# Six Strassen groups a layer instead of four, their split differences in slots of their own, and a 512-wide first product in every Strassen tile

## The chip, the cores and the metric

The kernel runs on one core of a Trainium2 chip. The time is that of one execution in device microseconds; the median of three executions of the kernel before is 1974.74 us (1974.21 to 1976.4). The core has a matrix engine (PE, which multiplies, and whose weight loads the profile lists apart as PEld), a vector engine (DVE), a scalar engine (ACT), GpSimd (POOL) and SyncE (SP), which here issues the loads of the weights.

## The reference, cut to what matters

Two layers over 256 tokens of width 2048: a recurrent block or an attention block, and behind each a SwiGLU block, the part that the change touches:

```python
D_MODEL = 2048; SEQ = 256
D_FF = 5632

def swiglu_ffn(x, g, w_in, w_out):
    h = rms_norm(x, g)
    gate, up = jnp.split(h @ w_in, 2, axis=-1)
    return x + (jax.nn.silu(gate) * up) @ w_out
```

All is float32. The kernel multiplies in a narrower format and keeps float32 precision by splitting each operand in a high and a low part and adding three products: high x high, high x low, low x high.

## The kernel before, in words

**Jobs.** The program is one list of jobs, one for each 512 KB tile of weights (256 rows by 512 columns). `stream` (line 321) walks through it: SP loads the tile of job i+4 into one of four `raw` buffers, ACT writes its high part `hi` and DVE its low part `lo` three jobs ahead (`split`, lines 295 to 310), and the job then issues its matmuls. `hi0..3`, `lo0..3` are here called the ring. The order of a job list and of the work between jobs (generators stepped by `run_bg` against budgets for DVE and ACT) is fixed when the program is built.

**Plain jobs** (`group`, `products`, matmul on line 375) have a ring tile as weights and the activations as moving operand; the activations (high and low part, 256 tokens each) lie in slots `s`. A plain job is 24 matmuls, each 256 columns wide. In groups whose output has a PSUM bank for itself, high x high and high x low can be issued as one matmul 512 wide whose two halves are added later; `products` does so in runs of three (a job then has 21 matmuls, three of them wide).

**Strassen jobs** (`strassen`, matmul on line 476) serve the first `NS` = 4 of the 22 groups of the SwiGLU input projection, eight jobs each. Operands are exchanged: the activations are the weights of the array, and the tile of the layer's weights moves. A job forms 7 products of 256 columns instead of 8, with three matmuls each: 21. Three products take a quarter of the ring tile as it is (`B(1)`, `B(3)`, `B(2)`); four take the differences t1 to t4, which POOL computes (`sums`, lines 279 to 281), ACT and DVE split in high and low two jobs ahead (`split_sums`, lines 289 and 291), and which lie in two sets of six slots taken from the pool of 58. In the first and last job of a group the products stand in the order of `todo`; in the six between, the three plain ones come first. Behind the eighth job `fast` (line 675) adds up the four banks on DVE, `task` applies SiLU and issues four transposes on PE through `pe_other` (lines 383 and 386), and `later` keeps the result back until the layer's last Strassen job is issued.

**Order of the jobs of one layer's input projection** (end of `ffn`): 8 plain jobs, then one Strassen job and two plain jobs in turn, then the rest of the plain ones; behind them the output projection. While they alternate, the plain jobs are of the kind without wide matmuls.

The weights are laid out for the Strassen groups on the host by `quarters`, with `NS` groups. Elsewhere in the program, the job of the shared K/V (lines 1052 to 1063) has twelve matmuls with operands as in a plain job, then twelve with operands exchanged as in a Strassen job.

Of the kernel before, what the change touches and what calls it, by code (L numbers as in the profile page):

```python
# [12 lines left out]
F32 = mybir.dt.float32  # L13
F32R = mybir.dt.float32r
AF = mybir.ActivationFunctionType
ALU = mybir.AluOpType

P = 128
D = 2048
T = 256  # L20
DFF = 5632
ND = D // P
# [19 lines left out]
class Val:  # L42


    def __init__(self, ap=None):
        self.ap = ap
        self.ready = False


class Trunk:  # L50
# [15 lines left out]
    DVE_TICK = 640.0  # L66
    ACT_TICK = 800.0

    NS = 4
    AHEAD = 8  # L70
    OWN = 2
    LS = 2
# [2 lines left out]
    def __init__(self, ctx, tc, dram):  # L75
        self.tc, self.nc, self.d = tc, tc.nc, dram
        nc = self.nc
        const = ctx.enter_context(tc.tile_pool(name="const", bufs=1))
        psum = ctx.enter_context(tc.tile_pool(name="psum", bufs=1, space=bass.MemoryType.PSUM))
        tmp = ctx.enter_context(tc.tile_pool(name="tmp", bufs=1))  # L80
        self.tmp = tmp
        self.par = const.tile([P, NPAR], F32, name="par")
        self.con = const.tile([P, NCON], F32, name="con")
        self.cc = const.tile([P, 32], F32, name="cc")
        self.x = [const.tile([P, 4, T], F32, name=f"x{i}") for i in range(4)]
        self.slots = deque(range(58))
        self.spool = const
        self.held = {}
        self.raw = [const.tile([P, 1024], F32, name=f"raw{i}") for i in range(4)]
        self.hi = [const.tile([P, 1024], F32R, name=f"hi{i}") for i in range(4)]  # L90
        self.lo = [const.tile([P, 1024], F32R, name=f"lo{i}") for i in range(4)]
        self.banks = deque(psum.tile([P, 512], F32, name=f"b{i}") for i in range(8))
        self.misc = 0
        self.started = False
        self.xin = 0
        self.other = None
        self.summing = False
        self.opening = None
        self.sets = None
        self.runs = 0  # L100
        self.since = 0
        self.hold = False
        self.tmps = deque(const.tile([P, T], F32, name=f"t{i}") for i in range(4))
        self.halves = deque(const.tile([P, T], F32, name=f"h{i}") for i in range(8))
        self.rstd = [const.tile([P, T + 2], F32, name=f"rstd{i}") for i in range(2)]
        self.acc = const.tile([P, T], F32, name="acc")
        self.sq = deque(const.tile([P, T], F32, name=f"sq{i}") for i in range(2))
        self.jobs = []
        self.bg = deque()
        self.tick = -2 * self.LD  # L110
        self.dve = 0.0
        self.act = 0.0
# [17 lines left out]
    def tt(self, out, a, b, op):  # L130
        self.dve += 69 + 1.042 * self._n(out)
        self.nc.vector.tensor_tensor(out, a, b, op)  # L132
# [14 lines left out]
        self.nc.vector.reciprocal(out, a)  # L147


    def slot(self, dt=F32R):  # L150
        i = self.slots.popleft()
        s = self.spool.tile([P, 2 * T], dt, tag=f"s{i}", name=f"s{i}")
        self.held[id(s)] = (i, s)
        return s

    def free(self, s):
        self.slots.append(self.held.pop(id(s))[0])

    def half(self):
        if self.halves:  # L160
# [108 lines left out]
    def sums(self, i):  # L269

        raw, tt = self.raw[i % 4], self.nc.gpsimd.tensor_tensor
        if not self.sets:
            self.sets = deque([self.slot(F32), self.slot(F32)] + [self.slot() for _ in range(4)] for _ in range(2))
        s = self.sets.popleft()
        self.sets.append(s)
        self.jobs[i][2]["set"] = s
        b = raw[:, :].rearrange("p (b t) -> p b t", b=4)
        two = lambda q: q.rearrange("p (b t) -> p b t", b=2)
        tt(two(s[0][:, :]), b[:, 0:3:2, :], b[:, 1::-1, :], ALU.subtract)  # L279
        tt(s[1][:, 0:T], raw[:, 2 * T:3 * T], s[0][:, 0:T], ALU.subtract)  # L280
        tt(s[1][:, T:2 * T], raw[:, 3 * T:4 * T], s[1][:, 0:T], ALU.subtract)  # L281
# [39 lines left out]
    def stream(self):  # L321
        n = len(self.jobs)
        self.warm()
        for i in range(-self.LD, n):
            self.tick = 2 * i
            if i + self.LD < n:
                self.load(i + self.LD)
            if 0 <= i + self.LC < n:
                self.split(i + self.LC)
            if 0 <= i + self.LS < n:  # L330
                self.split_sums(i + self.LS)
            if i >= 0:
                self.jobs[i][1](self.hi[i % 4], self.lo[i % 4])
            else:
                self.half_tick()
            self.run_bg()
        self.drain()
# [108 lines left out]
    def strassen(self, src, xs, forms, done, last, left):  # L446

        st = {}
        jobs = []
        for c in range(ND // 2):  # L450
            part = {}

            def mm(hi, lo, c=c, part=part):
                if c == 0:
                    st["ps"] = [self.bank() for _ in range(4)]
                    st["begun"] = set()
                ps = st["ps"]
                x2 = [self.need(xs[2 * c + kt]) for kt in range(2)]
                fh, fl = self.need(forms[c])
                A = lambda kt, b: tuple(x2[kt][:, q + b * P:q + b * P + P] for q in (0, T))  # L460
                S = lambda n: tuple(q[:, n * P:n * P + P] for q in (fh, fl))
                B = lambda n: tuple(q[:, n * T:n * T + T] for q in (hi, lo))
                s = part["set"]
                t1, t3, t2, t4 = (tuple(s[n + q][:, h * T:h * T + T] for q in (0, 1)) for n in (2, 4) for h in range(2))
                todo = [(0, 0, A(0, 0), B(1)), (1, 1, A(1, 0), B(3)), (1, 0, S(1), t2), (2, 0, S(0), t1),
                        (2, 1, S(2), t3), (3, 0, S(3), B(2)), (3, 1, A(1, 1), t4)]
                if 0 < c < ND // 2 - 1:
                    todo = [todo[q] for q in (0, 1, 5, 3, 4, 2, 6)]
                if self.other is not None:
                    self.runs = self.RUNS  # L470
                    self.other = None
                for n, (b, h, w, m) in enumerate(todo):
                    if n == 4:
                        self.half_tick()
                    for i, j in ((0, 0), (0, 1), (1, 0)):
                        self.nc.tensor.matmul(ps[b][:, h * T:h * T + T], w[i], m[j], start=b not in st["begun"],  # L476
                                              stop=c == ND // 2 - 1 and i == 1, skip_group_check=True)
                        st["begun"].add(b)
                        self.since += 1
                left[0] -= 1  # L480
                if last and c == ND // 2 - 1:
                    for q in self.sets:
                        for t in q:
                            self.free(t)
                    self.sets = None
                if last:
                    for q in (fh, fl):
                        self.free(q)
                if c == ND // 2 - 1:
                    done(ps)  # L490
            jobs.append((src(c), mm, part))
        return jobs

# [160 lines left out]
    def ffn(self, l, xs, forms, r, gains, rn, out=None):  # L654
        hid = [Val() for _ in range(NH)]
        w = self.d[f"ffn_in{l}"]
        one = self.con[:, K_ID:K_ID + P]
        turns, ordinary = [], []
        left = [self.NS * ND // 2]

# [12 lines left out]

        for g in range(self.NS):
            def fast(ps, g=g):
                c1, U, V = self.t(), self.slot(F32), self.slot(F32)
                two = lambda q: q.rearrange("p (b t) -> p b t", b=2)
                twice = lambda q: q.unsqueeze(1).broadcast_to([P, 2, T])
                self.a(c1, ps[0][:, 0:T])
                self.tt(two(U[:, :]), two(ps[1][:, :]), twice(c1[:, :]), ALU.add)  # L680
                self.tt(two(V[:, :]), two(ps[2][:, :]), twice(U[:, 0:T]), ALU.add)
                self.tt(U[:, 0:T], ps[2][:, 0:T], V[:, T:2 * T], ALU.add)
# [4 lines left out]
                def task():  # L687
# [23 lines left out]
                    yield from later(g, s)  # L711
                self.spawn(task())
            turns += self.strassen(lambda c, g=g: w[g, c], xs, forms, fast, g == self.NS - 1, left)
        for g in range(self.NS, NH // 2):
            def done(ps, g=g):
# [4 lines left out]
                def task():  # L720
# [28 lines left out]
                    if both is not None:  # L749
                        yield from later(g, both)  # L750
                self.spawn(task())
            self.group(lambda c, g=g: w[g, c], ND, xs, done, g == NH // 2 - 1, self.SYNC,
                       paired=2 * (g <= (self.OWN + 1) * self.NS), jobs=ordinary)
        n = len(turns)
# [618 lines left out]
```

## Time and profile before

| | |
|---|---|
| median of three executions | 1974.74 us |
| the profiled execution's own time | 1976.51 us |
| its span | 1974.7 us |
| granted TensorE clock | 1.00 (share of full speed) |
| PE, PEld busy | 100%, 98% |
| DVE, ACT, POOL busy | 72%, 57%, 19% |
| weights read | 372 MB, 189 GB/s over the span |

Matmuls overlap, so the mean duration of one in the page (282 ns for line 476) is not what it adds to the time. What it adds is the distance from its start to the next start; the chain of work that ended last gives it, where a piece of n matmuls follows another without a gap. A row of the chain reads: start in us, length in us, engine, tile, line, number of instructions.

### The profile page before, as it was taken

What the parts mean: (1) busy time and instruction counts of PE and PEld (TensorE: products, weight loads), DVE (VectorE), ACT (ScalarE), POOL (GpSimd) and SP (SyncE); (2) the same over time, 40 slices, a digit from 0 to 9 for tenths busy, and PEclk for the clock granted to TensorE, in tenths of its full rate; (3) what the DMA queues carried; (4) which work ended last, traced back from release to release, by engine and by line L of the source; (5) the groups of instructions that cost most, each with busy time, mean ns of one, the idle gap of its engine ahead of it and who ended that gap; (6) DMA issues with size and microseconds to landing.
All of it is one profiled execution on the core that took longest, in us unless ns stands there. A gap on an engine that the chain in (4) does not pass through costs nothing.

```text
span 1974.7 us, 40978 instructions
## 1 busy us (share of the span) xinstructions
PE 1966.7 (100%) x16762; PEld 1934.6 (98%) x16762; DVE 1428.8 (72%) x2073; ACT 1121.2 (57%) x1746; POOL 383.4 (19%) x356
## 2 busy tenths in 40 slices
PE   9999999999999999999999999999999999999999
PEld 9999999999999999999999889999999999999999
DVE  8988978988986655545668767888889665554443
ACT  6798766555555444434556776655556554444442
POOL 0000125555520000000002454354444000000000
PEclk9999999999999999999999999999999999999999
DMA  8555665665555555555555434565555656556664
GB/s 276 187 190 177 200 209 193 187 208 197 192 201 191 195 193 192 193 193 196 195 185 182 129 129 152 191 214 193 193 193 201 194 193 193 194 196 205 206 205 127
DMA packets 106204, 377.16 MB, mean 191 GB/s; under 512 B 11936, under 2 KB 14368, under 8 KB 106016
## 3 DMA queue, kind: packets, MB, share of 16 engines
q1 hardware_dynamic: 105408, 373.88, 57.7%
q8 instruction: 131, 2.15, 0.4%
q10 hardware_dynamic: 608, 0.66, 0.1%
q14 instruction: 57, 0.47, 0.1%
HBM read 371.88 MB, written 2.10 MB: 189 GB/s over the span
## 4 chain that ended last, share of the span: by engine, by line
PE 96%; DVE 2%; ACT 1%; issue 0%; POOL 0%; DMA 0%; ACTq 0%; DVEq 0%; POOLq 0%
PE b L375 84%; PE b L476 8%; PE b L386 1%; PE b L866 1%; PE b L383 1%; ACT s L123 1%; DVE lo L309 1%; PE b L1052 1%; ACT hi L306 0%; DVE s L1120 0%; DVE s L132 0%; DMA x<-in_x 0%; PE b L1061 0%; PE b L1062 0%; PE b L1063 0%
## 5 line engine op out<-in xcount | busy, mean ns | idle before, releaser
L375 PE MATMUL b<-s,hi 128*128 128x256 f32 (+1 forms) x9536 | 1301.0, 282 | 1.6 <-ACT s L123 1.0
L375 PEld LDWEIGHTS b<-s,hi 128*128 128x128 f32 x9536 | 1203.1, 188 | 21.4 <-ACT s L123 1.7
L309 DVE TENSOR_TENSOR lo<-raw,hi 128x1024 fp32r<-128x1024 f32 (+1 forms) x643 | 812.5, 1266 | 447.4 <-ACT hi L306 444.8
L306 ACT ACTIVATE hi<-raw 128x1024 fp32r<-128x1024 f32 (+1 forms) x643 | 676.0, 1054 | 588.6 <-PE b L375 508.1
L375 PE MATMUL b<-s,lo 128*128 128x256 f32 x4992 | 748.3, 277 | 0.0
L375 PEld LDWEIGHTS b<-s,lo 128*128 128x128 f32 x4992 | 651.0, 188 | 0.5
L279 POOL TENSOR_TENSOR s<-raw 128x512 f32<-128x512 f32 x64 | 120.8, 1888 | 233.3 <-DMA raw<-in_ffn_in 185.6
L291 DVE TENSOR_TENSOR s<-s,s 128x512 fp32r<-128x512 f32 x128 | 141.5, 1141 | 0.6 <-ACT s L289 0.3
L1142 POOL TENSOR_TENSOR s<-s 128x128 f32<-128x128 f32 x32 | 14.7, 462 | 537.0 <-ACT s L123 534.3
L476 PE MATMUL b<-s,s 128*128 128x256 f32 x768 | 105.6, 282 | 0.5 <-DVE s L291 0.5
L299 ACT ACTIVATE hi<-raw 128x768 fp32r<-128x768 f32 x64 | 54.1, 845 | 78.8 <-PE b L375 56.5
L476 PEld LDWEIGHTS b<-s,s 128*128 128x128 f32 x768 | 97.3, 189 | 0.8 <-DVE s L291 0.7
L123 ACT ACTIVATE s<-s 128x256 fp32r<-128x256 f32 (+3 forms) x180 | 69.1, 429 | 33.4 <-POOL s L508 19.5
L132 DVE TENSOR_TENSOR s<-s,s 128x256 fp32r<-128x256 f32 (+3 forms) x148 | 70.6, 509 | 19.8 <-ACT s L123 19.7
L476 PE MATMUL b<-hi,s 128*128 128x256 f32 x384 | 80.7, 281 | 0.0
L280 POOL TENSOR_TENSOR s<-raw,s 128x256 f32<-128x256 f32 x64 | 78.7, 1230 | 5.0
L300 DVE TENSOR_TENSOR lo<-raw,hi 128x768 fp32r<-128x768 f32 x64 | 70.5, 1102 | 12.6 <-PE b L375 8.1
L289 ACT ACTIVATE s<-s 128x512 fp32r<-128x512 f32 x128 | 73.6, 617 | 7.8 <-POOL s L281 7.8
L506 POOL TENSOR_TENSOR s<-s 128x128 f32<-128x128 f32 x16 | 14.0, 877 | 328.8 <-ACT s L123 328.8
L281 POOL TENSOR_TENSOR s<-raw,s 128x256 f32<-128x256 f32 x64 | 70.9, 1108 | 5.0
L476 PEld LDWEIGHTS b<-hi,s 128*128 128x128 f32 x384 | 64.6, 189 | 0.0
L123 ACT ACTIVATE s<-x,par 128x256 fp32r<-128x256 f32 (+1 forms) x112 | 52.6, 498 | 19.9 <-DVE x L132 13.5
(121 smaller groups left out, 1127.4 us busy)
## 6 DMA issues: line engine op xcount, KB each, us to landing
raw<-in_ffn_in SPq DMA_DIRECT2D x352, 512.0 KB, 3.5
raw<-in_ffn_out SPq DMA_DIRECT2D x176, 512.0 KB, 3.4
raw<-in_lru_in SPq DMA_DIRECT2D x62, 512.0 KB, 3.6
raw<-in_lru_out SPq DMA_DIRECT2D x32, 512.0 KB, 3.8
raw<-in_w_q SPq DMA_DIRECT2D x32, 512.0 KB, 3.4
raw<-in_w_o SPq DMA_DIRECT2D x32, 512.0 KB, 3.3
raw<-in_gate SPq DMA_DIRECT2D x8, 512.0 KB, 3.7
raw<-in_kv SPq DMA_DIRECT2D x8, 512.0 KB, 3.4
```

The source lines that it names most:

```text
L123: self.nc.scalar.activation(out, in_, func, **kw)
L132: self.nc.vector.tensor_tensor(out, a, b, op)
L279: tt(two(s[0][:, :]), b[:, 0:3:2, :], b[:, 1::-1, :], ALU.subtract)
L280: tt(s[1][:, 0:T], raw[:, 2 * T:3 * T], s[0][:, 0:T], ALU.subtract)
L281: tt(s[1][:, T:2 * T], raw[:, 3 * T:4 * T], s[1][:, 0:T], ALU.subtract)
L289: self.nc.scalar.activation(a, z, AF.Copy)
L291: self.nc.vector.tensor_tensor(b, z, a.bitcast(F32), ALU.subtract)
L300: low = self.nc.vector.tensor_tensor(lo[:, q], raw[:, q], hi[:, q].bitcast(F32), ALU.subtract)
L306: high = self.ins(self.nc.scalar.activation(hi[:, q], raw[:, q], AF.Copy))
L309: low = self.nc.vector.tensor_tensor(lo[:, q], raw[:, q], hi[:, q].bitcast(F32), ALU.subtract)
L375: self.nc.tensor.matmul(*args, **kw)
L476: self.nc.tensor.matmul(ps[b][:, h * T:h * T + T], w[i], m[j], start=b not in st["begun"], stop=c == ND // 2 - 1 and i == 1, skip_group_ch ...
```

## The change: what it does

Three things. `NS` goes from 4 to 6, so per layer 48 instead of 32 jobs are Strassen jobs, and 128 instead of 144 plain. The eight slots of the split differences come from a deque of their own (`odd`), which lies in memory right behind the ring, while the pool shrinks from 58 to 57 slots; `hi` and `lo` of a ring tile become the two halves of one tile `part`. All tiles keep their address modulo 512 bytes but these eight: the slots `s` begin at 32 modulo 512, the ring and now the eight slots at 480. The room comes from a scratch area at the start of the memory, which goes from 16 KB to 2 KB a partition. And the first product of a Strassen job, high x high and high x low, is one matmul 512 wide into both halves of its bank; `fast` adds the halves with one more DVE operation.

```diff
--- before.py
+++ after.py
@@ -66,7 +66,10 @@
     DVE_TICK = 640.0
     ACT_TICK = 800.0
 
-    NS = 4
+    NS = 6
+    SLOTS = 57
+    ODD = 8
+    SCRATCH = 2048
     AHEAD = 8
     OWN = 2
     LS = 2
@@ -83,12 +86,15 @@
         self.con = const.tile([P, NCON], F32, name="con")
         self.cc = const.tile([P, 32], F32, name="cc")
         self.x = [const.tile([P, 4, T], F32, name=f"x{i}") for i in range(4)]
-        self.slots = deque(range(58))
+        self.slots = deque(range(self.SLOTS))
+        self.odd = deque(range(self.SLOTS, self.SLOTS + self.ODD))
         self.spool = const
         self.held = {}
         self.raw = [const.tile([P, 1024], F32, name=f"raw{i}") for i in range(4)]
-        self.hi = [const.tile([P, 1024], F32R, name=f"hi{i}") for i in range(4)]
-        self.lo = [const.tile([P, 1024], F32R, name=f"lo{i}") for i in range(4)]
+        self.parts = [const.tile([P, 2, 1024], F32R, name=f"part{i}") for i in range(4)]
+        self.hi, self.lo = ([q[:, h, :] for q in self.parts] for h in range(2))
+        for i in self.odd:
+            const.tile([P, 2 * T], F32R, tag=f"s{i}", name=f"s{i}")
         self.banks = deque(psum.tile([P, 512], F32, name=f"b{i}") for i in range(8))
         self.misc = 0
         self.started = False
@@ -147,14 +153,15 @@
         self.nc.vector.reciprocal(out, a)
 
 
-    def slot(self, dt=F32R):
-        i = self.slots.popleft()
+    def slot(self, dt=F32R, odd=False):
+        i = (self.odd if odd else self.slots).popleft()
         s = self.spool.tile([P, 2 * T], dt, tag=f"s{i}", name=f"s{i}")
         self.held[id(s)] = (i, s)
         return s
 
     def free(self, s):
-        self.slots.append(self.held.pop(id(s))[0])
+        i = self.held.pop(id(s))[0]
+        (self.slots if i < self.SLOTS else self.odd).append(i)
 
     def half(self):
         if self.halves:
@@ -270,7 +277,7 @@
 
         raw, tt = self.raw[i % 4], self.nc.gpsimd.tensor_tensor
         if not self.sets:
-            self.sets = deque([self.slot(F32), self.slot(F32)] + [self.slot() for _ in range(4)] for _ in range(2))
+            self.sets = deque([self.slot(F32), self.slot(F32)] + [self.slot(F32R, True) for _ in range(4)] for _ in range(2))
         s = self.sets.popleft()
         self.sets.append(s)
         self.jobs[i][2]["set"] = s
@@ -330,6 +337,7 @@
             if 0 <= i + self.LS < n:
                 self.split_sums(i + self.LS)
             if i >= 0:
+                self.i = i
                 self.jobs[i][1](self.hi[i % 4], self.lo[i % 4])
             else:
                 self.half_tick()
@@ -462,6 +470,7 @@
                 B = lambda n: tuple(q[:, n * T:n * T + T] for q in (hi, lo))
                 s = part["set"]
                 t1, t3, t2, t4 = (tuple(s[n + q][:, h * T:h * T + T] for q in (0, 1)) for n in (2, 4) for h in range(2))
+                pair = self.parts[self.i % 4][:, :, T:2 * T]
                 todo = [(0, 0, A(0, 0), B(1)), (1, 1, A(1, 0), B(3)), (1, 0, S(1), t2), (2, 0, S(0), t1),
                         (2, 1, S(2), t3), (3, 0, S(3), B(2)), (3, 1, A(1, 1), t4)]
                 if 0 < c < ND // 2 - 1:
@@ -472,7 +481,12 @@
                 for n, (b, h, w, m) in enumerate(todo):
                     if n == 4:
                         self.half_tick()
-                    for i, j in ((0, 0), (0, 1), (1, 0)):
+                    if n == 0:
+                        self.nc.tensor.matmul(ps[0][:, :].rearrange("p (b t) -> p b t", b=2), w[0], pair,
+                                              start=c == 0, stop=c == ND // 2 - 1, skip_group_check=True)
+                        st["begun"].add(0)
+                        self.since = 0
+                    for i, j in ((0, 0), (0, 1), (1, 0))[2 * (n == 0):]:
                         self.nc.tensor.matmul(ps[b][:, h * T:h * T + T], w[i], m[j], start=b not in st["begun"],
                                               stop=c == ND // 2 - 1 and i == 1, skip_group_check=True)
                         st["begun"].add(b)
@@ -676,7 +690,8 @@
                 c1, U, V = self.t(), self.slot(F32), self.slot(F32)
                 two = lambda q: q.rearrange("p (b t) -> p b t", b=2)
                 twice = lambda q: q.unsqueeze(1).broadcast_to([P, 2, T])
-                self.a(c1, ps[0][:, 0:T])
+                self.a(c1, ps[0][:, T:2 * T])
+                self.tt(c1, ps[0][:, 0:T], c1, ALU.add)
                 self.tt(two(U[:, :]), two(ps[1][:, :]), twice(c1[:, :]), ALU.add)
                 self.tt(two(V[:, :]), two(ps[2][:, :]), twice(U[:, 0:T]), ALU.add)
                 self.tt(U[:, 0:T], ps[2][:, 0:T], V[:, T:2 * T], ALU.add)
@@ -1360,7 +1375,8 @@
         arr[f"ffn_in{l}"] = quarters(tiles(wi), Trunk.NS)
         arr[f"ffn_out{l}"] = tiles(ffn_w_out[l])
 
-    nc = bacc.Bacc("TRN2", target_bir_lowering=False, num_devices=1)
+    nc = bacc.Bacc("TRN2", target_bir_lowering=False, num_devices=1,
+                   dynamic_dma_scratch_size=Trunk.SCRATCH)
     dram = {n: nc.dram_tensor(f"in_{n}", v.shape, F32, kind="ExternalInput").ap() for n, v in arr.items()}
     dram["out"] = nc.dram_tensor("out_y", (P, ND, T), F32, kind="ExternalOutput").ap()
     with tile.TileContext(nc) as tc:
```

On PE, one Strassen job of the first layer stood so before (line, operation, output bank <- operands, columns; `hi_77` and `lo_81` are a ring tile, `s_38xx` split differences, the other `s` activations), in the rows up to the first products with a difference:

```order
L375 MATMUL b_84<-s_3262,lo_80 128x256 x2
L476 MATMUL b_85<-hi_77,s_3211 128x256
L476 MATMUL b_85<-lo_81,s_3211 128x256
L476 MATMUL b_85<-hi_77,s_3211 128x256
L476 MATMUL b_86<-hi_77,s_3225 128x256
L476 MATMUL b_86<-lo_81,s_3225 128x256
L476 MATMUL b_86<-hi_77,s_3225 128x256
L476 MATMUL b_88<-hi_77,s_3334 128x256
L476 MATMUL b_88<-lo_81,s_3334 128x256
L476 MATMUL b_88<-hi_77,s_3335 128x256
L476 MATMUL b_87<-s_3869,s_3334 128x256
```

The same place of the changed program (`part_76` is the ring tile with both parts):

```order
L383 MATMUL b_88<-s_3525,part_75 128x256 x2
L485 MATMUL b_89<-part_76,s_3249 128x512
L490 MATMUL b_89<-part_76,s_3249 128x256
L490 MATMUL b_90<-part_76,s_3266 128x256 x3
L490 MATMUL b_92<-part_76,s_3342 128x256 x2
L490 MATMUL b_92<-part_76,s_3343 128x256
L490 MATMUL b_91<-s_3879,s_3342 128x256
```

Two matmuls of 256 columns have become one of 512; the order of the products is the same.

On DVE, between two Strassen groups of the second layer, the rows from the low part of a plain tile before `fast` to the split of the differences for the next group's first job were (`b` is a bank of the group that has ended):

```order
L300 TENSOR_TENSOR lo_79<-raw_71,hi_75 128x768
L132 TENSOR_TENSOR s_16079<-b_90,t_91 128x512
L132 TENSOR_TENSOR s_16080<-b_83,s_16079 128x512
L132 TENSOR_TENSOR s_16079<-b_83,s_16080 128x256
L132 TENSOR_TENSOR s_16080<-b_86,s_16080 128x512
L309 TENSOR_TENSOR lo_80<-raw_72,hi_76 128x1024
L136 SCALAR_TENSOR_TENSOR s_16080<-s_16080,rstd_104,s_16079 128x256
L136 SCALAR_TENSOR_TENSOR s_16079<-s_16079,rstd_104,s_16080 128x256
L291 TENSOR_TENSOR s_14591<-s_14588,s_14590 128x512
L291 TENSOR_TENSOR s_14593<-s_14589,s_14592 128x512
```

In the changed program they are:

```order
L307 TENSOR_TENSOR part_75<-raw_71,part_75 128x768
L138 TENSOR_TENSOR t_97<-b_91,t_97 128x256
L138 TENSOR_TENSOR s_16139<-b_88,t_97 128x512
L138 TENSOR_TENSOR s_16140<-b_94,s_16139 128x512
L138 TENSOR_TENSOR s_16139<-b_94,s_16140 128x256
L138 TENSOR_TENSOR s_16140<-b_92,s_16140 128x512
L316 TENSOR_TENSOR part_76<-raw_72,part_76 128x1024
L142 SCALAR_TENSOR_TENSOR s_16140<-s_16140,rstd_108,s_16139 128x256
L142 SCALAR_TENSOR_TENSOR s_16139<-s_16139,rstd_108,s_16140 128x256
L298 TENSOR_TENSOR s_14666<-s_14663,s_14665 128x512
L298 TENSOR_TENSOR s_14668<-s_14664,s_14667 128x512
```

One operation of 256 columns is added at the head of `fast`; all else follows in the same order. In the second layer four transposes stand inside the first Strassen job of the next group, before and after; in the first layer they stood inside the second plain job ahead of the second Strassen job, and now stand right ahead of the first one.

## The prediction

> **What bounds the kernel now.** I read the page's busy times and chain first, then the chain of the stretch in which Strassen and plain jobs alternate, piece by piece.
>
> ```profile
> PE 1966.7 (100%) x16762; PEld 1934.6 (98%) x16762; DVE 1428.8 (72%) x2073; ACT 1121.2 (57%) x1746; POOL 383.4 (19%) x356
> PE 96%; DVE 2%; ACT 1%; issue 0%; POOL 0%; DMA 0%; ACTq 0%; DVEq 0%; POOLq 0%
> ```
>
> PE is busy all the time and carries 96% of the chain, so what counts is how many matmuls PE issues and how far apart. Here is the chain of the first layer around the boundary between two Strassen groups:
>
> ```profile
> 421.28 2.49 PE b L476 x21
> 423.77 5.44 PE b L375 x48
> 429.22 2.49 PE b L476 x21
> 431.71 5.44 PE b L375 x48
> 437.15 2.48 PE b L476 x21
> 439.63 5.65 PE b L375 x48
> 445.29 2.46 PE b L476 x21
> 447.75 4.25 PE b L375 x36
> 451.99 0.11 PE b L383
> 452.10 0.33 PE b L386 x3
> 452.43 1.42 PE b L375 x12
> 453.85 2.45 PE b L476 x21
> ```
>
> No piece waits for another engine, yet matmuls of equal width differ. A plain job's step is 5.44/48 = 113.3 ns. A Strassen job's is 2.49/21 = 118.6 ns. And behind the last job of a group (439.63) and its successor's first (447.75) the same plain jobs take 5.65/48 = 117.7 ns and 4.25/36 = 118 ns, until the next Strassen job. So a stream of matmuls runs at a short step (113.3) or at a long one (118), and a Strassen job can hand over either. The job of the shared K/V shows the rule without the differences. Twelve matmuls with weights from the ring (L1052) alternate with twelve with the ring as the moving operand (L1061 to L1063):
>
> ```profile
> 1011.28 0.12 PE b L1061
> ...
> 1012.69 1.41 PE b L1052 x12
> 1014.11 0.12 PE b L1061
> ...
> 1015.48 1.36 PE b L1052 x12
> 1016.84 0.12 PE b L1061
> ...
> 1018.26 1.41 PE b L1052 x12
> ```
>
> From start to start, the exchanged twelve take 1.41 us (long step), 1.37 (short), 1.42 (long), and the plain twelve behind them 1.41, 1.36, 1.41. So both kinds can run at the short step, the plain stream inherits the step of the exchanged one, and passing from plain to exchanged flips it. In a Strassen job only 9 of 21 matmuls are of the exchanged kind; in 12 both operands lie in slots. After the change all are exchanged, as far as the place modulo 512 bytes goes.
>
> **The change part by part.** The sum is made against the profiled execution, 1976.5 us with a span of 1974.7, 1.8 us above the median of the runs shown.
>
> *Fewer and dearer jobs.* Per layer 16 plain jobs become Strassen jobs. 32 x 2.72 us (half of 5.44) = 87.0 us go. The old 64 Strassen jobs cost 64 x 2.48 = 158.7 us (five of a group's eight at 2.49, the others 2.48, 2.46, 2.45). The new price needs a wide matmul, which stands in the chain only in plain jobs, three in this piece:
>
> ```profile
> 33.12 5.56 PE b L375 x46
> ```
>
> 5.56 - 43 x 0.1133 = 0.69 us, 0.23 each. No row has one with exchanged operands; bounds are two narrow ones, 0.227 at the short step and 0.237 at the long one, +-0.5 us over 96 jobs. At the short step a job is 0.23 + 19 x 0.1133 = 2.38 us and 96 of them 228.7. Net: -87.0 - 158.7 + 228.7 = **-17.0 us**.
>
> *The plain jobs at the long step.* At a boundary they cost 0.21 + 0.17 + 0.06 = 0.44 us over the short one. That is three boundaries a layer and the two jobs behind the last Strassen job: 6 x 0.44 + 2 x 0.21 = **-3.1 us** if every Strassen job now hands over the short step. The whole stretch agrees:
>
> ```profile
> 316.94:567.99 251.06, 251.06 (x2174) 251.00 (x2173) 229.06 (x249) 143.30 (x208) 133.72 (x91) 1.00 0.60 196
> 567.99:791.00 223.01, 223.01 (x1869) 219.04 (x1868) 135.77 (x189) 108.12 (x145) 0.00 (x0) 1.00 0.59 195
> ```
>
> 62 plain jobs at 2.72, 32 Strassen jobs at 2.48 and three times 0.44 us for the transposes (452.43 - 451.99) make 249.3; the 1.7 us left are the stretch's plain jobs at the long step.
>
> Does one wide matmul bring the job to the short step? It takes twice the time of a narrow one for one weight load, so what the loads lag behind the matmuls in the plain stream should be gone when the second product starts; the exchanged twelve at 1014.11 show that exchanged operands can then stay at it. The range is between the short step everywhere and the long one everywhere: 19 + 48 matmuls at +4.5 ns, 0.30 us a Strassen job, 29 us in all. I take the short step, the end to which the K/V rows with exchanged operands (1.37) and their plain heirs (1.36) are nearest.
>
> A rule speaks against the placement. The Trainium skill says, on "TensorE: Matmul & The Clock Gate", section "Step-by-step: what each phase is for", that loading the next tile's weights "doesn't steal SBUF read bandwidth from the running matmul", over two independent read ports. By it, where the operands lie could change nothing, and the steps above would be equal; the trace disagrees (118.6 against 113.3 ns at one width), but it doesn't say which of place, order and width is the cause.
>
> *Four more groups.* Each brings four transposes, 0.44 us with the restart: **+1.8 us**.
>
> *DVE at the boundary.* `fast` has one more DVE operation. The rows of a boundary in the second layer, DVE and then the chain:
>
> ```profile
> 1336.26 1.95 DVE L132 TENSOR_TENSOR s<-b,s 128x512 f32<-128x512 f32 x3
> 1338.12 1.89 DVE L309 TENSOR_TENSOR lo<-raw,hi 128x1024 fp32r<-128x1024 f32 x1
> 1339.93 1.83 DVE L136 SCALAR_TENSOR_TENSOR s<-s,rstd,s 128x256 f32<-128x256 f32 x2
> 1341.69 1.28 DVE L291 TENSOR_TENSOR s<-s,s 128x512 fp32r<-128x512 f32 x2
> 1344.03 1.41 DVE L132 TENSOR_TENSOR h<-b,rstd 128x256 f32<-128x256 f32 x4
> ```
> ```profile
> 1336.77 5.65 PE b L375 x48
> 1342.43 1.46 PE b L476 x12
> ```
>
> DVE works through without a gap and ends the differences of the next group's first job at 1341.69 + 1.28 = 1342.97. PE needs the second pair after six matmuls, at 1342.43 + 0.71 = 1343.14: 0.17 us to spare. The added operation costs 0.35 us (a quarter of 1.41), and PE arrives 0.21 us earlier (5.44 for 5.65). The wait is then 0.35 + 0.21 - 0.17, some 0.4 us; I take 0.5 at each of five boundaries, +2.5. Queued on PE behind the waiting product are the rest of its job and two plain jobs; all come later by it, and ACT's and DVE's next splits, which wait for PE, with them. A wait in mid-job may also leave the stream at the long step until the next wide one (0.30 us; I take half of five, +0.75). Together **+3.2 us**; the bounds are 0 (PE so far late that the operation hides) and 1 us at all ten boundaries. In the first layer the transposes now stand ahead of that job and give DVE 0.44 us, so I charge nothing there.
>
> *Costed at nothing.* 38 instead of 26 halves held by `later` are split behind the last Strassen job, within 24 plain jobs (65 us). DVE is 61% busy in the second window above, so 25 us are free against 38 x 0.35 = 13; if that cover were gone, PE would wait at the output projection for up to the difference. The jobs with three wide matmuls become 35 fewer, each saving 3 x (0.23 - 0.227): **-0.2 us** at most. The pool of 57 slots loses one but is freed of eight set tiles, and holds two more results and four more held groups. The scratch: the trace shows these queues with data,
>
> ```profile
> q1 hardware_dynamic: 105408, 373.88, 57.7%
> q10 hardware_dynamic: 608, 0.66, 0.1%
> ```
>
> and SP's transfers keep order and size; no row shows the scratch in use, so I charge nothing; the loads fill 0.60 of the DMA time in the stretch and would cost only if they slowed by half. The Trainium skill ("DMA: Bandwidth & Descriptors", section "SWDGE vs HWDGE vs iDMA") puts there the descriptor rings of transfers issued by GpSimd, of which this kernel has none; no run here shows it.
>
> Sum: -17.0 - 3.1 + 1.8 + 3.2 - 0.2 = **-15.3 us**, so 1961.2 for an execution like the profiled one, and 1959.5 beside the median.
>
> **The rivals.**
> - *The wide matmul resets nothing.* Then the K/V rule holds: each pass from plain to exchanged flips, and every second Strassen job with its two plain jobs runs at the long step: 48 x 0.30 = +14.5 us, 1974. For it: the rows at 1011 to 1018. Against: there no wide one stands between.
> - *It lands at the long step each time.* The 96 jobs and the 192 plain ones behind them run at 118: +29 us, **1988, slower**. It decides from the point at which 15.3/0.30 = 51 of the 96 jobs are at the long step. For it: today's six middle jobs are at it in every pass, so each job can repeat the last. Against: those end with matmuls that have both operands in slots, and no such one is left.
> - *DVE becomes the bound.* It is busy 229.06 of 251.06 us in the stretch, 91%, and a cycle shrinks from 7.93 to 7.82 us while its work grows. On average that still fits, but with waits of 1.2 us at all ten boundaries there are 12 us in place of the 3.2: 1968.
> - *The placement and the wide matmul do nothing* (the skill's rule): the job stays at 2.48 us and the plain ones as they are: -87.0 + 32 x 2.48 = -7.6, with the long step at four more boundaries +1.8, transposes +1.8, DVE +3.2: 1974.
>
> **How the numbers follow.** Forecast 0.62; flipping 0.11; long step each time 0.11; DVE 0.10; nothing 0.06. A measurement of this kernel can tell some 0.2%, 4 us, from no change. Forecast and DVE are faster by more: 0.72. Flipping and nothing lie within: 0.17. The long step each time is slower: 0.11. The range takes in the forecast without any DVE wait (1956) and with the cheaper wide matmul (1955), and reaches up over the DVE case and the two at 1974 to 1976; only the case at 1988 is left out.
>
> **What would show it.** In the chain of the changed kernel a Strassen job of 20 matmuls should take 2.38 us and the 48 behind it 5.44, at the boundaries too. 2.48 and 5.65 in every second pass would be the flip, in each pass the long step throughout; 2.48 with 5.44 would mean that the placement does nothing. The page's row of the products with a difference shows PE's wait for their split,
>
> ```profile
> L476 PE MATMUL b<-s,s 128*128 128x256 f32 x768 | 105.6, 282 | 0.5 <-DVE s L291 0.5
> ```
>
> and its 0.5 us should rise to some 3, in the second layer alone; a wait at the start of the output projection, or loads that land late, would make the costs set at nothing wrong.

## The result, and the profile after

The changed kernel takes 1964.44 us (median of four executions, 1963.69 to 1964.86) against 1974.78 for the kernel before beside it: a ratio of 0.9946, with a 95% interval of 0.9932 to 0.996. The profiled executions are 1964.86 and 1976.51 us. So the change brings 10 to 12 us where 15.3 was forecast. First the page of the changed kernel: busy times, shares of the chain, and the rows of the products with a difference (line 490 now, and line 298 for the split that they wait for).

```profile
PE 1951.8 (99%) x16691; PEld 1917.9 (98%) x16691; DVE 1500.8 (76%) x2125; ACT 1140.9 (58%) x1794; POOL 526.8 (27%) x452
PE 92%; DVE 4%; ACT 1%; issue 1%; POOL 1%; DMA 0%; DVEq 0%; ACTq 0%; POOLq 0%
L490 PE MATMUL b<-s,s 128*128 128x256 f32 x1152 | 155.0, 278 | 3.9 <-DVE s L298 3.7
L490 PEld LDWEIGHTS b<-s,s 128*128 128x128 f32 x1152 | 141.2, 188 | 5.9 <-DVE s L298 5.8
```

PE's share of the chain fell from 96% to 92% and DVE's rose from 2% to 4%: stretches have appeared in which PE stands and DVE is what ends last. Now the chain of the changed kernel around a group boundary of the first layer. A Strassen job is a piece of one wide matmul (L485) and a piece of 19 (L490).

```profile
427.02 0.23 PE b L485
427.25 2.16 PE b L490 x19
429.41 5.44 PE b L383 x48
...
437.24 5.44 PE b L383 x48
...
445.10 5.45 PE b L383 x48
450.54 0.11 PE b L391
450.65 0.33 PE b L394 x3
450.98 0.23 PE b L485
451.21 2.24 PE b L490 x19
453.45 5.65 PE b L383 x48
459.11 0.23 PE b L485
459.34 2.17 PE b L490 x19
461.51 5.44 PE b L383 x48
```

From 427.02 to 429.41 a job takes 2.39 us (2.49 before), and the 48 plain matmuls behind it 5.44. Behind the last job of a group (437.24) they take 5.44, which was 5.65, and behind the first job of the next group (445.10) 5.45, also at the short step. The four transposes of the first layer (450.54) thus stand right ahead of the second Strassen job of the next group, and not ahead of its first, as the text on the change and the prediction have it. That second job (451.21) still hands the long step to its plain jobs (453.45), and the next wide matmul ends that. Of all 96 pairs of plain jobs behind Strassen jobs, 5 run at the long step.

The matrix engine's list of waits holds what was given back. Its columns are the engine, what waited for what, us in total, number of waits, the longest. Before, the same wait (L476 for L291) was 0.7 us, once, at the start of the second layer's stretch.

```profile
PEld b L490 <- DVE s L298: 5.8, 10, 1.1
```

That is 5.1 us more than before, where the forecast had 2.5. One of the ten waits is the old one, and four are at the boundaries of the second layer. Here is one of these, in the chain of the changed kernel:

```profile
1521.95 1.07 DVE part L316
...
1523.09 2.40 DVE s L142 x2
1525.48 0.22 DVE s L298
...
1526.55 0.69 DVE s L298
...
1527.28 0.74 PE b L490 x4
```

DVE works through a ring split (L316), then the old group's two gating products (L142), and only then the split of the next group's first differences (L298), for which PE stands until 1527.28. The other five come in the last Strassen group of a layer, where none was forecast. DVE's timeline there, in the first layer (start, length, engine, line, operation, tiles, shapes, count), and the piece of the chain that it ends in:

```profile
641.53 0.42 DVE L138 TENSOR_TENSOR s<-s,s 128x256 fp32r<-128x256 f32 x1
...
642.79 3.23 DVE L138 TENSOR_TENSOR s<-s,s 128x256 fp32r<-128x256 f32 x3
645.95 2.31 DVE L316 TENSOR_TENSOR part<-raw,part 128x1024 fp32r<-128x1024 f32 x1
648.18 2.37 DVE L298 TENSOR_TENSOR s<-s,s 128x512 fp32r<-128x512 f32 x2
...
672.44 2.93 DVE L298 TENSOR_TENSOR s<-s,s 128x512 fp32r<-128x512 f32 x2
```
```profile
674.15 1.23 DVE s L298
...
675.42 0.86 PE b L490 x5
```

The rows `s<-s,s 128x256 fp32r` on L138 are low parts of halves held by `later`. The last Strassen job of the layer runs at 690, yet these splits run from 637 on: in each layer the trace has 28 of them from the start of the last eight Strassen jobs to the end of the last one. (The kernel before had 22 there.) DVE has no room for them, being busy for 34.5 of the 36 us from 640 to 676, and PE stands for the row at 672.44 until 675.42.

### The profile page after: what moved, and what is told of

The parts are those of the page before. It is cut to its first block, busy times and chain, and to the rows that moved or that the text cites. A ratio compares the mean times of both kernels' runs of the same rounds, so it can differ in the third digit from the quotient of the medians.

```text
span 1963.1 us, 41116 instructions
## 1 busy us (share of the span) xinstructions
PE 1951.8 (99%) x16691; PEld 1917.9 (98%) x16691; DVE 1500.8 (76%) x2125; ACT 1140.9 (58%) x1794; POOL 526.8 (27%) x452
## 4 chain that ended last, share of the span: by engine, by line
PE 92%; DVE 4%; ACT 1%; issue 1%; POOL 1%; DMA 0%; DVEq 0%; ACTq 0%; POOLq 0%
PE b L383 77%; PE b L490 9%; PE b L394 2%; DVE part L316 1%; PE b L881 1%; DVE s L138 1%; PE b L485 1%; PE b L391 1%; DVE s L142 1%; DVE s L298 1%; PE b L1067 1%; ACT s L129 0%; ACT part L313 0%; DVE part L307 0%; POOL s L286 0%
## 5 line engine op out<-in xcount | busy, mean ns | idle before, releaser
L383 PE MATMUL b<-s,part 128*128 128x256 f32 (+1 forms) x13864 | 1642.0, 279 | 1.5 <-DVE h L138 0.8
L383 PEld LDWEIGHTS b<-s,part 128*128 128x128 f32 x13864 | 1614.5, 188 | 17.8 <-ACT s L129 1.5
L316 DVE TENSOR_TENSOR part<-raw,part 128x1024 fp32r<-128x1024 f32 (+1 forms) x611 | 788.2, 1293 | 346.8 <-ACT part L313 343.7
L313 ACT ACTIVATE part<-raw 128x1024 fp32r<-128x1024 f32 (+1 forms) x611 | 641.4, 1053 | 474.6 <-PE b L383 388.1
L286 POOL TENSOR_TENSOR s<-raw 128x512 f32<-128x512 f32 x96 | 187.5, 1953 | 338.9 <-DMA raw<-in_ffn_in 287.3
L298 DVE TENSOR_TENSOR s<-s,s 128x512 fp32r<-128x512 f32 x192 | 205.5, 1106 | 7.9 <-ACT s L296 7.8
L490 PE MATMUL b<-s,s 128*128 128x256 f32 x1152 | 155.0, 278 | 3.9 <-DVE s L298 3.7
L490 PEld LDWEIGHTS b<-s,s 128*128 128x128 f32 x1152 | 141.2, 188 | 5.9 <-DVE s L298 5.8
L306 ACT ACTIVATE part<-raw 128x768 fp32r<-128x768 f32 x96 | 80.9, 843 | 97.4 <-PE b L383 75.5
L287 POOL TENSOR_TENSOR s<-raw,s 128x256 f32<-128x256 f32 x96 | 120.0, 1250 | 7.5
L307 DVE TENSOR_TENSOR part<-raw,part 128x768 fp32r<-128x768 f32 x96 | 102.6, 1069 | 20.4 <-PE b L383 16.9
L288 POOL TENSOR_TENSOR s<-raw,s 128x256 f32<-128x256 f32 x96 | 106.7, 1112 | 7.5
L138 DVE TENSOR_TENSOR s<-s,s 128x256 fp32r<-128x256 f32 (+3 forms) x172 | 82.5, 508 | 21.0 <-ACT s L129 20.5
L490 PEld LDWEIGHTS b<-part,s 128*128 128x128 f32 x672 | 92.4, 188 | 4.1
L490 PE MATMUL b<-part,s 128*128 128x256 f32 x672 | 95.9, 276 | 0.0
L138 DVE TENSOR_TENSOR h<-b,rstd 128x256 f32<-128x256 f32 x128 | 46.9, 412 | 0.1
```

The lines of the kernel that those rows point to most:

```text
L298: self.nc.vector.tensor_tensor(b, z, a.bitcast(F32), ALU.subtract)
L307: low = self.nc.vector.tensor_tensor(lo[:, q], raw[:, q], hi[:, q].bitcast(F32), ALU.subtract)
L313: high = self.ins(self.nc.scalar.activation(hi[:, q], raw[:, q], AF.Copy))
L316: low = self.nc.vector.tensor_tensor(lo[:, q], raw[:, q], hi[:, q].bitcast(F32), ALU.subtract)
L383: self.nc.tensor.matmul(*args, **kw)
```

## The experiments

The theory behind all of them: the wide matmul and the slots beside the ring together make the short step; what was lost against the forecast are waits for DVE, half of them at the second layer's boundaries and half from held halves split too early. The rivals: either edit alone does it, or neither; the two waits are one; more groups are the whole gain. Ratios are to the kernel before, with their 95% intervals.

**e1: the wide matmul undone.** Line 490 becomes 485 here.

```diff
-                    if n == 0:
-                        self.nc.tensor.matmul(ps[0][:, :].rearrange("p (b t) -> p b t", b=2), w[0], pair,
-                                              start=c == 0, stop=c == ND // 2 - 1, skip_group_check=True)
-                        st["begun"].add(0)
-                        self.since = 0
-                    for i, j in ((0, 0), (0, 1), (1, 0))[2 * (n == 0):]:
+                    for i, j in ((0, 0), (0, 1), (1, 0)):
...
-                self.a(c1, ps[0][:, T:2 * T])
-                self.tt(c1, ps[0][:, 0:T], c1, ALU.add)
+                self.a(c1, ps[0][:, 0:T])
```

> The changed kernel with the first plain product as three 256-wide matmuls again (and fast reading its first plane in one operation, as before); the slots of the differences stay beside the ring. Theory (the wide matmul sets the short step, without it each pass from plain to exchanged flips): every second Strassen job with its two plain jobs at the long step, mean job 2.43 us, half of the plain pairs at 5.65, some +15 us less 2 to 3 us of waits, since fast has one DVE operation fewer: 1975 to 1980 us. Rival (the wide one only replaces two narrow ones): job 2.38, plain pairs 5.44, 1961 to 1965 us.

1973.09 us, 0.999 (0.9982 to 0.9999). The chain shows the flip, pass by pass:

```profile
460.26 2.48 PE b L485 x21
462.74 5.66 PE b L383 x48
468.39 2.39 PE b L485 x21
470.79 5.44 PE b L383 x48
```

Jobs of 2.48 and 2.39 us alternate, and the plain jobs follow them with 5.65 and 5.44. Counted over the trace, 44 jobs and 42 pairs of plain jobs run at the long step, where the changed kernel had 5 such pairs: 44 x 0.09 + 37 x 0.21 = 11.7 us. The time rose by only 8.7, below what was expected. Most of the difference are the waits for DVE, which shrank from 5.8 to 1.6 us with a slower PE and one DVE operation fewer:

```profile
PEld b L485 <- DVE s L298: 1.6, 4, 0.7
```

**e2: the slots of the differences where all other slots lie.**

```diff
+        const.tile([P, 16], F32, name="pad")
         for i in self.odd:
             const.tile([P, 2 * T], F32R, tag=f"s{i}", name=f"s{i}")
+        const.tile([P, 112], F32, name="pad2")
```

> The changed kernel with 64 bytes put in front of the eight slots of the differences, so that they lie at 32 modulo 512 like all other slots (448 bytes behind them keep the rest in place); the wide product stays. Theory (12 of a job's 20 matmuls would have both operands at one place modulo 512 and run at 118 to 120 ns, whatever comes before): job 2.45 to 2.49 us, +6 to +10 us from the 96 jobs, and up to +20 more where the plain pairs inherit the long step: 1970 to 1990 us. Rival (where operands lie does nothing): job 2.38, 1964 us.

1970.19 us, 0.9975 (0.9966 to 0.9984), the low end of what was expected. Its chain (L487 is the wide matmul, L492 the rest, L385 the plain ones):

```profile
466.99 0.23 PE b L487
467.22 2.21 PE b L492 x19
469.43 5.44 PE b L385 x48
```

From 466.99 to 469.43 a job takes 2.44 us for 2.39, which is 96 x 0.05, some 5 us. By the starts of the single matmuls, those that follow the wide one with a ring tile as operand come 113 ns apart, as in the changed kernel, and the twelve with both operands in slots 118 to 119. So the wide matmul sets the short step at the head of the job whatever the place, and the place decides whether the rest of the job keeps it. The plain jobs behind a group's middle jobs stay at the short step, as they did before the change; but 23 of the 96 pairs run at the long one, 21 of them behind the first or last job of a group. That is 18 more than in the changed kernel, 3.8 us, against which the waits for DVE fell from 5.8 to 3.3.

**e9: both undone, six groups kept** (the edits of e1 and e2 together).

> Six groups without the slots beside the ring and without the wide product (both edits of e1 and e2): more groups and the small scratch alone. Theory (the Strassen job stays at 2.49 us, the plain jobs behind the last job of each group at the long step): -87.0 + 32 x 2.49 = -7.3, +1.8 for the long step at four more boundaries, +1.6 for their transposes, about +2 of waits on DVE: 1972 to 1974 us. Rival (the job takes 2.39 in any case, so that neither edit was needed): 1965 us or less.

1972.1 us, 0.9985 (0.9976 to 0.9994), and the job of the kernel before (468.82):

```profile
468.82 2.49 PE b L487 x21
```

More groups alone bring 3 us. Adding the slots alone changes that by +1.0 us (e1), adding the wide product alone by -1.9 (e2), adding both by -7.7. Neither is of much use without the other.

**e5: both edits, four groups.**

```diff
-    NS = 6
+    NS = 4
```

> The kernel meant by the fourth run: the changed kernel with four groups a layer in place of six, so slots beside the ring, the wide product and the small scratch alone. Theory (64 jobs at 2.39 for 2.487 give -6.4 us, the plain jobs at the long step -3.1, three boundary waits in the second layer give back 2): 1966 to 1968.5 us, so that the two added groups a layer are worth some 3 us net of their waits, of the 7 to 8 that jobs and transposes alone would give. Rival (the gain is the 32 cheaper jobs alone): 1974 us.

1969.17 us, 0.9969 (0.9958 to 0.9981): the edits alone bring 5.8 us, a little less than expected, and the two more groups of a layer 4.7 on top. That is less than the 32 x (2.72 - 2.39) = 10.6 us of their jobs less 1.8 for their transposes; most of the rest are the waits, 1.7 us here and 5.8 with six groups:

```profile
PEld b L490 <- DVE s L298: 1.7, 4, 0.6
```

**e4** carries an expectation for four groups, but the kernel under this label isn't that one: its edit is the limit on runs of three wide matmuls in plain jobs (`RUNS`, 3 to 4), with six groups.

```diff
-    RUNS = 3
+    RUNS = 4
```

> The changed kernel with four groups a layer in place of six: slots beside the ring, the wide product and the small scratch alone, without more groups. Theory (64 jobs at 2.38 for 2.487 give -6.5 us, the plain jobs at the long step -3.1, the extra DVE operation gives back 1.5 to 3 at three boundaries of the second layer): 1966 to 1968 us, and the two added groups a layer are then worth only 2 to 4 us. Rival (the gain is the 32 cheaper jobs, and the steps bring nothing): 1974 us.

1962.69 us, 0.994 (0.9928 to 0.9952), which its interval doesn't tell from the changed kernel. It says nothing on the number of groups; e5 does.

**e3: the held halves split behind the last Strassen job.** Each operation of the split is queued behind the ring's last split on its engine.

```diff
-                self.split_act(q, s[:, h * T:h * T + T])
+                src = s[:, h * T:h * T + T]
+                with self.tc.issue_after(self.behind[0]):
+                    self.a(q[:, 0:T], src)
+                with self.tc.issue_after(self.behind[1]):
+                    self.tt(q[:, T:2 * T], src, q[:, 0:T].bitcast(F32), ALU.subtract)
```

> The changed kernel with each split of a held half put behind the ring's last split on ACT and DVE, so that none of them stands among a layer's last eight Strassen jobs (31 do in the first layer, 36 in the second). Theory (these splits fill DVE and make PE wait for the differences in the last group: 1.9 us at 640 to 676 and 1.2 us at 1629 to 1647, and 0.5 us of plain jobs at the long step behind them): those waits go and nothing else moves, 1960.5 to 1961.5 us. Rival (POOL's subtractions, which take up to 6.3 us there, or the weights that land late make the wait): 1963.5 to 1965 us. If the splits come too late for the output projection: above 1966 us with a wait at its start.

1961.8 us, 0.9931 (0.9919 to 0.9943). The median fell by 2.6 us where 3 to 4 were expected, and by itself the interval doesn't tell the two kernels apart; the list of waits does:

```profile
PEld b L490 <- DVE s L298: 3.0, 5, 0.9
```

Five waits and 2.8 us are gone, all those of the last groups, and with them three of the five pairs of plain jobs at the long step. No wait of the output projection took their place.

**e6: the gating products behind the split of the differences.** `summed` is the last DVE operation of `split_sums`.

```diff
-                    yield
+                    yield 3
                     for q, k, s in ((V, U, 0), (U, V, 1)):
-                        self.stt(q[:, 0:T], q[:, 0:T], rs[s], k[:, T:2 * T], ALU.mult, ALU.mult)
+                        with self.tc.issue_after(self.summed):
+                            self.stt(q[:, 0:T], q[:, 0:T], rs[s], k[:, T:2 * T], ALU.mult, ALU.mult)
```

> The changed kernel with the two gating products of a Strassen group (two DVE operations of a boundary) put behind the split of the differences of the next group's first job. Theory (in the second layer these two stand ahead of that split and take 1.84 us there; they and the added operation make PE wait 0.6, 0.6, 1.0, 1.2 and 0.1 us at the five boundaries): the waits fall under 0.1 us each, the plain jobs at 1401 lose their long step, 1960.5 to 1961.5 us. Rival (DVE has no slack there, so the wait moves to a later job): within 1 us of the changed kernel.

1959.88 us, 0.9924 (0.991 to 0.9937).

```profile
PEld b L490 <- DVE s L298: 3.2, 7, 0.9
```

2.6 us of waits are gone, those at the boundaries of the second layer; what is left is in the last groups and at the stretch's start. No counted pair of plain jobs is left at the long step. The edit does a second thing: with it the four transposes come later, inside a plain job, in the second layer too, and this run doesn't tell what that alone is worth.

**e7: e3 and e6 together.**

> The edits of the runs e3 and e6 together. Theory (two separate waits): the gains add up, some 7 us less than the changed kernel, 1957 to 1959 us, and the wait of PE on the split of the differences falls to about 1 us, that at the start of each stretch. Rival (one wait took the place of the other): 1960 to 1962 us.

1958.95 us, 0.9916 (0.9903 to 0.993), faster than both kernels of this document. PE is back at 95% of the chain (the page's shares by engine), and one wait is left (the matrix engine's list), the one that the kernel before has as well:

```profile
PE 95%; DVE 2%; ACT 2%; issue 0%; POOL 0%; DMA 0%; ACTq 0%; DVEq 0%; POOLq 0%
```
```profile
PEld b L490 <- DVE s L298: 0.8, 1, 0.8
```

So there were two waits, not one that moves. Of the expected 7 us the medians show 5.5. The start of an execution adds scatter to such differences: e3's profiled execution came to its first Strassen job 2.3 us before that of the changed kernel (314.4 for 316.7), e7's 0.4 us before it (316.3), and e7's span is 6.3 us shorter (1956.8 for 1963.1). Without the start, from the first to the end of the last Strassen job of each layer, the two stretches add up to 753.3 us in the changed kernel, 749.3 in e3, 750.7 in e6 and 747.5 in e7: 4.0 and 2.6 us alone, 5.8 together.

**e8: e7 with seven groups**, and **e12: the same without the edit of e3.**

> e7 with seven groups a layer. Theory (PE is the bound once the waits are gone): 16 more plain jobs become Strassen jobs, -16 x (2.72 - 2.39) = -5.3 us, two more transposes +0.8: 4 to 5 us under e7, 1953 to 1954 us. Rival (no plain job is left behind the last Strassen job, so the held halves are split while the output projection waits for them): up to 16 us of splits a layer at its start, above e7 by 5 to 25 us.

> e8 without the edit of e3: seven groups, the gating products behind the split of the differences, and the held halves split where the program's order puts them, ahead of the last Strassen jobs too. Theory (the loss of e8 is that all held halves wait for the last Strassen job and then stand in front of the output projection): most of the 56 us are won back, but DVE still has more to do than it can in the last two groups: 1957 to 1966 us, no better than e7. Rival (seven groups by themselves overload DVE or POOL): above 1975 us.

e8: 2015.24 us, 1.02 (1.0186 to 1.0214). e12: 1965.43, 0.9947 (0.9931 to 0.9964). In e8 the plain jobs of the output projection wait for the high and low parts of the halves (PE's list of waits):

```profile
PE b L383 <- ACT s L129: 25.9, 15, 2.7
PE b L383 <- DVE s L138: 6.4, 7, 1.2
```

That was the rival, at more than twice the upper end of its price. With seven groups no plain job is left behind the last Strassen job, so the place behind it to which e3 moves the splits has no cover. Without that edit, 50 us come back, and seven groups are still no better than six: e3's place for the splits pays only with the 24 plain jobs at the end.

**e10: another place in memory.** 32 bytes in front of `x` put the ring at 0 and the slots at 64 modulo 512, in place of 480 and 32.

> e7 with 32 bytes put in front of x, so that the ring lies at 0 and the slots at 64 modulo 512 in place of 480 and 32: the distance between them stays, their place against 64 bytes changes. Theory (what counts is where the two operands of a matmul lie against each other): steps of 113.3 and 118 as before, 1957 to 1961 us. Rival (a place that is no multiple of 64 costs a cycle or two a matmul): a short step below 113 ns, and each ns less is worth some 14 us.

1958.44 us, 0.9917 (0.9901 to 0.9934), with e7's steps:

```profile
457.16 0.23 PE b L486
457.39 2.17 PE b L491 x19
459.56 5.44 PE b L384 x48
```

**e11: the small scratch alone, in the kernel before.**

> The kernel before with the 2 KB scratch alone; every tile moves down by 14336 bytes and keeps its place modulo 512. Theory (nothing uses the scratch): 1973.5 to 1976.5 us, the loads of the weights land as late as before. Rival (it is used, or the place in the memory matters): over 1 us away from the kernel before.

1974.82 us, 0.9998 (0.9989 to 1.0008): it costs and brings nothing.

## Why the prediction was right in direction and four to five microseconds too hopeful

The working, term by term, against the profiled executions (-15.3 forecast, -11.65 measured):

- *Fewer and dearer jobs, -17.0*: held. A job takes 2.39 us (427.02 to 429.41), forecast 2.38; over 96 jobs the rounding of these two hides up to 1 us, of which 0.4 is taken here. That it needs slots beside the ring and the wide matmul both is shown by e1, e2 and e9.
- *Plain jobs at the long step, -3.1*: held but for 5 pairs of jobs, 1.0 us; 0.75 us of that stood in the DVE term. The term left out the pair behind the first Strassen job of each layer, which ran at the long step before as well (5.65 us at 319.68 and at 1281.07 in that chain) and no longer does: 0.4 us more gained.
- *Four more groups' transposes, +1.8*: held: 450.54 to 450.98 is 0.44 us.
- *DVE at the boundary, +3.2*: right in place, and in size for the sum: the waits of the second layer's boundaries that e6 takes away are 2.6 us, forecast 2.5. The single ones run from about 0.1 to 1.1 us where 0.5 was taken for each, so the sum is in part luck. In the first layer, where nothing was charged, the list has no wait at a boundary either, but not for the reason given. The transposes stand behind the next group's first job, so they give its differences no time. What the first layer has instead is another order on DVE, in which the split of the differences (L298) comes ahead of the old group's gating products (L142), the order that e6 makes in the second layer:

```profile
440.81 2.37 DVE L298 TENSOR_TENSOR s<-s,s 128x512 fp32r<-128x512 f32 x2
...
445.56 0.47 DVE L142 SCALAR_TENSOR_TENSOR s<-s,rstd,s 128x256 f32<-128x256 f32 x1
```

- *Held halves, costed at nothing*: this is the step that failed. It said that 38 halves "are split behind the last Strassen job, within 24 plain jobs" and took DVE's free time from that window. The rows on L138 from 641 on show them among the last eight Strassen jobs, where DVE has next to none. e3 measures them: 2.8 us. Two things hid it. The text of `later` waits for the last Strassen job, but the program as built runs splits whose data are ready earlier; DVE's timeline of the kernel before shows the same rows there. And in that kernel 22 halves fitted in without a wait, 28 do not.

-15.3 + 0.4 - 0.4 + 0.3 + 2.8 = -12.2, within 0.6 us of the measured difference. The terms aren't known better than that: the old Strassen jobs were a little dearer than the 2.48 us taken for them (48 of them take 2.49), and of the new ones those beside transposes and waits take more than 2.39 (2.47 at 450.98). What is left between -12.2 and -11.65 is not shown apart.

The scratch, costed at nothing, is nothing (e11). Of the rivals, the flip is real but needs the wide matmul absent (e1). The long step in every pass didn't come: the 5.44 us behind the jobs are its refutation. DVE as the bound was half right: it is not the bound on average, but it is in the last group and at the second layer's boundaries. That neither the place nor the width matters is refuted by e2 and e1 against the changed kernel. That rival had the rule of the Trainium skill behind it ("TensorE: Matmul & The Clock Gate", "Step-by-step: what each phase is for"); a job of 2.44 us with both operands of twelve matmuls at one place, and 2.39 with them apart, is what this case has against it. Which of the chip's parts makes the difference isn't shown here.

## What to carry to other kernels

When PE is the bound, measure matmuls from start to start and look at what two neighbouring kinds of job hand on to each other: here two edits that bring 1.9 us and less than nothing apart gave 8 us together, since one set the step and the other kept it. When a term is costed at nothing because other work hides it, look up in the trace where that work stands in the engine's queue, not where the source emits it. An engine that is 76% busy overall can be full for the 30 us that count, and the cheapest cure is to move what nobody waits for behind what PE waits for.

## What the runs showed of the hardware

**POOL stretches DVE's work.** At the boundary of the changed kernel the two gating products take 2.40 us (1523.09). POOL subtracts all that time:

```profile
1522.71 1.61 POOL L286 TENSOR_TENSOR s<-raw 128x512 f32<-128x512 f32 x1 [5.90 <-DMA raw<-in_ffn_in]
1524.40 0.80 POOL L287 TENSOR_TENSOR s<-raw,s 128x256 f32<-128x256 f32 x1
1525.28 0.80 POOL L288 TENSOR_TENSOR s<-raw,s 128x256 f32<-128x256 f32 x1
```

In e7 the same two stand behind the differences' split, when POOL has been idle since 1521.73 (1520.66 + 1.07):

```profile
1519.90 2.38 DVE L298 TENSOR_TENSOR s<-s,s 128x512 fp32r<-128x512 f32 x2
...
1523.34 0.87 DVE L142 SCALAR_TENSOR_TENSOR s<-s,rstd,s 128x256 f32<-128x256 f32 x2
```
```profile
1520.66 1.07 POOL L288 TENSOR_TENSOR s<-raw,s 128x256 f32<-128x256 f32 x1
```

They take 0.87 us for 2.40. The Trainium skill ("SBUF — State Buffer", "Who interferes with whom") says that a DVE instruction with two inputs in this memory contends with a GpSimd instruction that reads from it, for one shared pair of ports. These rows agree (2.40 against 0.87 us). POOL's own times spread as well: its 128x512 subtraction took 1.61 us in the row above and 6.28 in the last group of the first layer. That DVE is what holds it up there is not shown apart:

```profile
637.69 6.28 POOL L286 TENSOR_TENSOR s<-raw 128x512 f32<-128x512 f32 x1 [5.24 <-DMA raw<-in_ffn_in]
```

So a Strassen group costs DVE more than its own operations wherever POOL's subtractions fall beside them. The prediction held this only as far as the boundary that it read had it, where the same two products took 1.83 us.

**The granted clock fell where PE paused.** In e8, while PE waits at the start of the output projection, the granted clock of the window is 0.84 (after the busy times); in every window of the changed kernel that was read it is 0.99 or 1.00.

```profile
735.00:800.00 65.00, 49.63 (x322) 45.81 (x320) 37.96 (x69) 30.71 (x63) 3.64 (x3) 0.84 0.39 129
```

In that window a piece of 19 matmuls takes 2.86 us at 766.31, at a granted clock of 1.00, and 4.26 us at 772.57, at 0.63. That fits e8's loss of 56 us where its list shows 32 us of waits for halves; how much of the rest is the clock wasn't measured apart.
